# HGRN2 scores below level 16: elementwise products and whole-block matmuls, or 32 keys on each column tile against their own 32 queries

## Chip, core and metric

One core of a Trainium2 chip runs the whole program. The time is the device time of one execution in microseconds; the runs shown are three executions, and one more was taken with the hardware profiler.

## What is computed

One decoder layer for a prompt of 256 tokens with 16 meta tokens ahead of it, and for 8 sample tokens: a half-step SwiGLU, a mixer, a second half-step SwiGLU, all in fp32. The mixer projects x by `w_in` into ten parts and runs two recurrences side by side, retention (8 heads) and HGRN2 (16 heads of 128). The change is in HGRN2's scores inside a block:

```python
b = jnp.cumsum(logf.astype(jnp.float32), axis=2)
causal = jnp.tril(jnp.ones((C, C), dtype=bool))
diff = b[:, :, :, None, :] - b[:, :, None, :, :]
decay = jnp.exp(jnp.where(causal[None, None, :, :, None], diff, -jnp.inf)).astype(q.dtype)
A = jnp.einsum('bhid,bhjd,bhijd->bhij', q, k, decay)
o = jnp.einsum('bhij,bhjv->bhiv', A, v) + jnp.einsum('bhid,bhdv->bhiv', q * jnp.exp(b).astype(q.dtype), S)
```

The decay depends on the query i, the key j and the channel d, so A is no plain matrix product. `f` is the forget gate, `logf` its logarithm, `k` is 1 - f.

## The kernel before

All large products run as three matmuls of rounded halves (`dense`, L217: xh by whi, xl by whi, xh by wlo). Weights stream in units of eight 128x128 blocks: SyncE (SP) issues the load `raw` (L184, three buffers), ScalarE rounds it to `whi` (L187), VectorE subtracts for `wlo` (L188). TensorE's order is the order of the code; the other engines' order is set by a scheduler from priorities and readiness, and each engine then runs its list in order.

In the mixer, `project()` walks the columns of `w_in` in groups of two outputs: 16 steps of six matmuls each, four steps to a weight unit. After every step `pump` counts down the waiting threads and lets those go on whose count is over. There are eight rounds u; round u starts one `mix_hg(u)` (two HGRN2 heads) and one `mix_ret(u)` (a retention head), generators whose `yield n` means: go on after n steps of the projection. Small matmuls thus stand between dense ones at places that the yields fix. `calm` adds two steps to most waits in u=2 to 6 and in u=0.

`mix_hg` splits a block's scores into levels 1 to 64. At level s, a key in the even half of a pair of s-token pieces meets a query in the odd half; before each level, K and Q are scaled by products T of forget gates (T1 is f, T2s is the product of neighbours in Ts), so that a product of K and Q has the right decay. The scores are put together in `acch`, keys on partitions.

- Diagonal, levels 1 and 2: products of columns of Q and K made by VectorE (`pr0` to `pr2`, then `pr0`, `pr1`), each rounded into two halves (`prodsmh`, `prodvbh`, ScalarE and VectorE), and summed over the 128 channels by a matmul with ones (`sums`, L236). The sums come out the same on all partitions; the diagonal is cut out by a product with the identity (L789), level 1 by one and level 2 by two masked copies (L883, `copy_predicated`).
- Levels 4 and 8: 128 keys by 192 columns of `Qm`, an arrangement of Q's odd halves with three scalings (L801), four fp32 matmuls, then six masked copies (L805).
- Levels 16, 32 (L825) and 64 (L820): small matmuls on column tiles (`tile_position=(0, j)`), copied by ScalarE.

After that come K's transposes (L899), the samples' state update (smh, vbh, L905 and L906), the states, the samples' products `pq` (L932, column tiles too) and the outputs. In `mix_ret` the names used below are `pt` (transposes, L1006), `vbr` and `smr` (the samples' values, broadcast by a load in two halves, `spread(0)` and `spread(1)`, and the samples' states, L1037 and L1069; `vbr` has one buffer) and `pqr` (L1083), the products with `smr`.

Of the kernel before, what the change touches and what calls it, by code (L numbers as in the profile page):

```python
# [14 lines left out]
ALU = mybir.AluOpType  # L15
# [32 lines left out]
MASKS = {1: [0], 2: [1, MASKED], 4: [2], 8: [3, MASKED + 1]}  # L48
# [79 lines left out]
def trunk(ctx: ExitStack, tc: tile.TileContext, A, O):  # L128
# [417 lines left out]
    with tc.tile_pool(name="yp", bufs=1) as yp:  # L546
# [7 lines left out]
        with tc.tile_pool(name="mp", bufs=1) as mp:  # L554
# [178 lines left out]
            def mix_hg(u, f, k, q, v):  # L733
# [51 lines left out]
                yield 9  # L785
                pd = mx_bank("pd")
                sums(pd, hilo, slice(0, 2))
                for h in range(2):
                    nc.vector.tensor_tensor(  # L789
                        out=acc[:, 2 * P * h : 2 * P * (h + 1)].rearrange("p (b c) -> p b c", b=2),  # L790
                        in0=pd.rearrange("p (b c h) -> p h b c", b=2, h=2)[:, h],
                        in1=ident.unsqueeze(1).to_broadcast([P, 2, P]), op=ALU.mult)
                Tt = f
                for s in LEVELS:
                    if s == 4:


                        for h in range(2):
                            pl = mx_bank("pl")
                            for b in range(2):  # L800
                                nc.tensor.matmul(  # L801
                                    pl[:, 192 * b : 192 * b + 192], K[:, h, NMETA + b * P : NMETA + b * P + P],
                                    Qm.rearrange("p i (x c) -> p i x c", x=4)[:, :, 2 * h + b, :], start=True, stop=True)
                            for i, (sl, mi) in enumerate(((4, MASKS[4][0]), (8, MASKS[8][0]), (8, MASKS[8][1]))):
                                nc.vector.copy_predicated(  # L805
                                    acc[:, 2 * P * h : 2 * P * (h + 1)].rearrange("p (b n t s) -> p b n t s", b=2, t=2, s=sl)[:, :, :, 1, :],
                                    msk[:, mi, :P].rearrange("p (b n s) -> p b n s", b=2, s=sl),
                                    pl[:, :384].rearrange("p (b i n s) -> p b i n s", b=2, i=3, s=sl)[:, :, i])
# [19 lines left out]

                    if s == NMETA:
                        Tt = Tt[:, :, 1:]  # L830
                    k0 = 0 if s < NMETA else NMETA
                    n = LP - k0
                    nb = n // s
                    m = nb // 2
                    t2 = Tt[:, :, :nb].rearrange("p h (n t) -> p h n t", t=2)
                    kv = K[:, :, k0:].rearrange("p h (n t s) -> p h n t s", t=2, s=s)
                    qv = Q.rearrange("p h (n t s) -> p h n t s", t=2, s=s)
                    mq = SEQ // (2 * s)
                    mul(kv[:, :, :, 0, :], kv[:, :, :, 0, :], t2[:, :, :, 1].unsqueeze(3).to_broadcast([P, 2, m, s]))
                    if s != 4:  # L840
                        mul(qv[:, :, :, 1, :], qv[:, :, :, 1, :], t2[:, :, m - mq :, 0].unsqueeze(3).to_broadcast([P, 2, mq, s]))
                    Tn = tmp(f"T{2 * s}", (P, 2, m))
                    mul(Tn, t2[:, :, :, 0], t2[:, :, :, 1])
                    Tt = Tn
# [44 lines left out]
                    if s != 4:  # L889
                        yield W_LEVEL + 2 * (s <= 2 or u == 1) + calm  # L890
# [358 lines left out]
```

## Time and profile before

| what | us |
| --- | --- |
| runs (three): median, lowest, highest | 2610.65, 2608.11, 2611.9 |
| profiled execution | 2608.88 |
| its span in the trace | 2607.1 |
| TensorE busy in the span | 2586.9 |
| VectorE, ScalarE busy | 1723.9, 1385.2 |
| granted TensorE clock, mean | 0.999 |

The profiled execution is 1.8 us longer than its span, and 1.8 us shorter than the median of the runs. A row of a timeline gives the start, the duration (a matmul's end is modelled, so neighbours overlap), engine, line, operation and operands, then a count of the records in the row.

### The profile page before, as it was taken

What the parts mean: (1) busy time and instruction counts of PE and PEld (TensorE: products, weight loads), DVE (VectorE), ACT (ScalarE), POOL (GpSimd) and SP (SyncE); (2) the same over time, 40 slices, a digit from 0 to 9 for tenths busy, and PEclk for the clock granted to TensorE, in tenths of its full rate; (3) what the DMA queues carried; (4) which work ended last, traced back from release to release, by engine and by line L of the source; (5) the groups of instructions that cost most, each with busy time, mean ns of one, the idle gap of its engine ahead of it and who ended that gap; (6) DMA issues with size and microseconds to landing.
All of it is one profiled execution on the core that took longest, in us unless ns stands there. A gap on an engine that the chain in (4) does not pass through costs nothing.

```text
span 2607.1 us, 54875 instructions
## 1 busy us (share of the span) xinstructions
PE 2586.9 (99%) x22744; PEld 2554.0 (98%) x22744; DVE 1723.9 (66%) x2907; ACT 1385.2 (53%) x2184; POOL 12.9 (0%) x62
## 2 busy tenths in 40 slices
PE   9999999999999999999999999999999999999999
PEld 9999999999999889999999999999999999999998
DVE  6454444565579787777777777776995555556555
ACT  5444444444456666766666666675564444444444
POOL 0000000000000000000000000000000000000000
PEclk9999999999999999999999999999999999999999
DMA  7555555555556676767676767666556666666664
GB/s 244 183 185 186 186 183 184 185 185 184 183 198 222 219 260 205 262 202 260 206 260 201 262 202 259 207 228 194 193 188 200 195 195 196 196 196 193 199 196 147
DMA packets 154587, 536.17 MB, mean 206 GB/s; under 512 B 17696, under 2 KB 25696, under 8 KB 154336
## 3 DMA queue, kind: packets, MB, share of 16 engines
q1 hardware_dynamic: 154048, 532.37, 63.1%
q8 instruction: 178, 2.92, 0.5%
q14 instruction: 73, 0.60, 0.1%
q10 hardware_dynamic: 288, 0.29, 0.0%
HBM read 501.99 MB, written 30.61 MB: 204 GB/s over the span
## 4 chain that ended last, share of the span: by engine, by line
PE 92%; DVE 4%; DMA 2%; ACT 2%; issue 1%; SPq 0%; POOL 0%; DVEq 0%; POOLq 0%; ACTq 0%
PE up L217 36%; PE dn L217 18%; PE pj_q_r L217 3%; PE wo L217 3%; PE pj_v_r L217 3%; PE pj_i_h L217 3%; PE pj_f L217 3%; PE pj_k_r L217 3%; PE pj_g_r L217 3%; PE pj_q_h L217 3%; PE pj_a_r L217 3%; PE pj_g_h L217 3%; PE pj_a_h L217 3%; DVE wlo L188 1%; DMA out_srp<-sro 1%; PE pqr L1083 1%
## 5 line engine op out<-in xcount | busy, mean ns | idle before, releaser
L188 DVE TENSOR_TENSOR wlo<-raw,whi 128x1024 fp32r<-128x1024 f32 (+1 forms) x869 | 1061.6, 1222 | 735.1 <-ACT whi L187 732.8
L187 ACT CAST whi<-raw 128x1024 fp32r<-128x1024 f32 (+1 forms) x870 | 905.5, 1042 | 906.5 <-PE up L217 415.2
L217 PE MATMUL up<-xh,wlo 128*128 128x280 f32 (+1 forms) x2624 | 725.7, 280 | 0.3 <-DVE wlo L188 0.3
L217 PE MATMUL up<-xh,whi 128*128 128x280 f32 (+1 forms) x2624 | 726.0, 280 | 0.0
L217 PE MATMUL up<-xl,whi 128*128 128x280 f32 (+1 forms) x2624 | 725.4, 279 | 0.0
L217 PEld LDWEIGHTS up<-xh,wlo 128*128 128x128 f32 x2624 | 492.6, 189 | 0.7 <-DVE wlo L188 0.7
L217 PEld LDWEIGHTS up<-xh,whi 128*128 128x128 f32 x2624 | 493.1, 189 | 0.0
L217 PEld LDWEIGHTS up<-xl,whi 128*128 128x128 f32 x2624 | 492.7, 189 | 0.0
L217 PE MATMUL dn<-hh,whi 128*128 128x280 f32 (+1 forms) x1376 | 384.7, 280 | 0.0
L217 PE MATMUL dn<-hl,whi 128*128 128x280 f32 (+1 forms) x1376 | 384.3, 279 | 0.0
L217 PE MATMUL dn<-hh,wlo 128*128 128x280 f32 (+1 forms) x1376 | 384.3, 279 | 0.0
L217 PEld LDWEIGHTS dn<-hh,whi 128*128 128x128 f32 x1376 | 260.1, 189 | 0.1
L217 PEld LDWEIGHTS dn<-hl,whi 128*128 128x128 f32 x1376 | 260.1, 189 | 0.1
L217 PEld LDWEIGHTS dn<-hh,wlo 128*128 128x128 f32 x1376 | 260.1, 189 | 0.0
L217 PE MATMUL pj_g_r<-xh,whi 128*128 128x264 f32 x256 | 76.7, 299 | 0.0
L217 PE MATMUL pj_v_r<-xh,whi 128*128 128x280 f32 x256 | 74.2, 290 | 0.0
L217 PE MATMUL pj_g_h<-xh,whi 128*128 128x264 f32 x256 | 73.5, 287 | 0.0
L217 PE MATMUL pj_v_r<-xh,wlo 128*128 128x280 f32 x256 | 72.4, 283 | 0.3 <-DVE wlo L188 0.3
L217 PE MATMUL pj_k_r<-xh,whi 128*128 128x280 f32 x256 | 72.7, 284 | 0.0
L217 PE MATMUL pj_k_r<-xh,wlo 128*128 128x280 f32 x256 | 72.4, 283 | 0.0
L217 PE MATMUL pj_v_r<-xl,whi 128*128 128x280 f32 x256 | 72.3, 283 | 0.0
L217 PE MATMUL pj_k_r<-xl,whi 128*128 128x280 f32 x256 | 72.3, 283 | 0.0
(403 smaller groups left out, 5283.4 us busy)
## 6 DMA issues: line engine op xcount, KB each, us to landing
raw<-in_w_up SPq DMA_DIRECT2D x343, 512.0 KB, 4.2
raw<-in_w_in SPq DMA_DIRECT2D x320, 512.0 KB, 4.0
raw<-in_w_dn SPq DMA_DIRECT2D x172, 512.0 KB, 3.5
smr<-in_sr SPq DMA_DIRECT2D x32, 512.0 KB, 5.6
out_srs<-smr SPq DMA_DIRECT2D x32, 512.0 KB, 4.8
raw<-in_w_out SPq DMA_DIRECT2D x32, 512.0 KB, 3.6
smh<-in_sg SPq DMA_DIRECT2D x16, 512.0 KB, 4.4
vbr<-vrd SPq DMA_DIRECT2D x16, 512.0 KB, 4.4
```

The costliest lines, as they stand in the source:

```text
L187: nc.scalar.copy(hi[:, j:jn, :], raw[:, j:jn, :])
L188: nc.vector.tensor_tensor(out=lo[:, j0:j1, :], in0=raw[:, j0:j1, :], in1=hi[:, j0:j1, :].bitcast(F32), op=ALU.subtract)
L217: nc.tensor.matmul(o, w, t, start=start, stop=stop)
L1083: nc.tensor.matmul(pq[32 * j : 32 * j + 32, :256], qdr[:, c, 32 * b : 32 * b + 32], sms[2 * e + c][:, j, :], start=e + c == 0, stop=e + c ...
```

## The change

Levels 1 and 2 with the diagonal, and levels 4 and 8, are each one call of `blocks()`. It takes 32 keys on the column tile (0, j) and multiplies them with the three 16-column arrangements of their own 32 queries (L808, 48 moving columns); the first call also with the 32 queries as they are, for the diagonal (L810, 32 columns). Each head's results lie in one bank and are taken by a product with the identity for the diagonal (L815, first call alone) and three masked copies of 128 elements a partition (L821). `side_by_side` (two ScalarE copies and two VectorE scalings) makes the arrangement for each call. K is scaled by f and T2 only after the first call, by T4 and T8 after the second. The products `pr`, their halves and `sums` over them are gone, and so is the extra wait of two steps after levels 1 and 2: the calls stand 14 and 27 steps after the start of the thread where `calm` is 2, level 16 at 39 as before. The two masks of level 2 change places in the table.

```diff
-MASKS = {1: [0], 2: [1, MASKED], 4: [2], 8: [3, MASKED + 1]}
+MASKS = {1: [0], 2: [MASKED, 1], 4: [2], 8: [3, MASKED + 1]}
...
-                hilo = [tmp("prod" + t, (P, 3, SEQ), dt=F32R, tag=t, bufs=2) for t in ("smh", "vbh")]
-                for i in range(3):
-                    pr = tmp(f"pr{i}", (P, SEQ))
-                    if i < 2:
-                        mul(pr, q[:, i, :SEQ], k[:, i, NMETA:LP])
-                    else:
-                        mul(pr.rearrange("p (h c) -> p h c", h=2), Q[:, :, 1::2], K[:, :, NMETA::2])
-                    split(hilo[0][:, i], hilo[1][:, i], pr)
+                Ts = {1: f}
+                def sides(s):
+                    k0 = 0 if s < NMETA else NMETA
+                    m = (LP - k0) // (2 * s)
+                    Tt = Ts[s] if k0 == 0 or s > NMETA else Ts[s][:, :, 1:]
+                    return k0, m, Tt[:, :, : 2 * m].rearrange("p h (n t) -> p h n t", t=2)
+                def scale_k(s):
+                    k0, m, t2 = sides(s)
+                    x = K[:, :, k0:].rearrange("p h (n t s) -> p h n t s", t=2, s=s)[:, :, :, 0, :]
+                    mul(x, x, t2[:, :, :, 1].unsqueeze(3).to_broadcast([P, 2, m, s]))
+                def odd(s):
+                    return Q.rearrange("p h (n t s) -> p h n t s", t=2, s=s)[:, :, :, 1, :]
+                def scale_q(s):
+                    _, m, t2 = sides(s)
+                    n = SEQ // (2 * s)
+                    mul(odd(s), odd(s), t2[:, :, m - n :, 0].unsqueeze(3).to_broadcast([P, 2, n, s]))
+                def join(s):
+                    _, m, t2 = sides(s)
+                    Ts[2 * s] = tmp(f"T{2 * s}", (P, 2, m))
+                    mul(Ts[2 * s], t2[:, :, :, 0], t2[:, :, :, 1])
+                def side_by_side(s):
+                    x = tmp("Qm", (P, 3, 2 * P), tag="smh", bufs=2)
+                    part = lambda i, s: x[:, i, :].rearrange("p (h n s) -> p h n s", h=2, s=s)
+                    nc.scalar.copy(part(0, s), odd(s))
+                    scale_q(s)
+                    nc.scalar.copy(part(1, 2 * s), odd(2 * s))
+                    k0 = NMETA // s
+                    t4 = Ts[s][:, :, k0 : k0 + SEQ // s].rearrange("p h (n t) -> p h n t", t=4)[:, :, :, 1]
+                    mul(part(2, 2 * s), odd(2 * s), t4.unsqueeze(3).to_broadcast([P, 2, SEQ // (4 * s), 2 * s]))
+                    return x
+                def blocks(x, s, own=None):
+                    x = x.rearrange("p i (x j c) -> p i x j c", x=4, j=4)
+                    for h in range(2):
+                        pl = mx_bank("pl")
+                        half = pl[:, : 2 * 80].rearrange("p (b c) -> p b c", b=2)
+                        for b in range(2):
+                            for j in range(0, P, 32):
+                                kk = K[:, h, NMETA + b * P + j : NMETA + b * P + j + 32]
+                                o = half[j : j + 32, b, :48].rearrange("p (i c) -> p i c", i=3)
+                                nc.tensor.matmul(o, kk, x[:, :, 2 * h + b, j // 32, :], start=True, stop=True, tile_position=(0, j))
+                                if own is not None:
+                                    nc.tensor.matmul(
+                                        half[j : j + 32, b, 48:], kk, own[:, h, b * P + j : b * P + j + 32],
+                                        start=True, stop=True, tile_position=(0, j))
+                        a = acc[:, 2 * P * h : 2 * P * (h + 1)]
+                        if own is not None:
+                            nc.vector.tensor_tensor(
+                                out=a.rearrange("p (b j c) -> p b j c", b=2, j=4),
+                                in0=half[:, :, 48:].unsqueeze(2).to_broadcast([P, 2, 4, 32]),
+                                in1=ident.rearrange("p (j c) -> p j c", j=4).unsqueeze(1).to_broadcast([P, 2, 4, 32]), op=ALU.mult)
+                        for i, (sl, mi) in enumerate(((s, MASKS[s][0]), (2 * s, MASKS[2 * s][0]), (2 * s, MASKS[2 * s][1]))):
+                            n = 16 // sl
+                            nc.vector.copy_predicated(
+                                a.rearrange("p (b j n t s) -> p b j n t s", b=2, j=4, t=2, s=sl)[:, :, :, :, 1, :],
+                                msk[:, mi, :P].rearrange("p (b j n s) -> p b j n s", b=2, j=4, s=sl),
+                                half[:, :, 16 * i : 16 * i + 16].rearrange("p b (n s) -> p b n s", s=sl).unsqueeze(2).to_broadcast([P, 2, 4, n, sl]))
+                join(1)
+                Q1 = side_by_side(1)
...
-                yield 9
-                pd = mx_bank("pd")
-                sums(pd, hilo, slice(0, 2))
-                for h in range(2):
-                    nc.vector.tensor_tensor(
-                        out=acc[:, 2 * P * h : 2 * P * (h + 1)].rearrange("p (b c) -> p b c", b=2),
-                        in0=pd.rearrange("p (b c h) -> p h b c", b=2, h=2)[:, h],
-                        in1=ident.unsqueeze(1).to_broadcast([P, 2, P]), op=ALU.mult)
-                Tt = f
-                for s in LEVELS:
-                    if s == 4:
-                        for h in range(2):
-                            pl = mx_bank("pl")
-                            for b in range(2):
-                                nc.tensor.matmul(
-                                    pl[:, 192 * b : 192 * b + 192], K[:, h, NMETA + b * P : NMETA + b * P + P],
-                                    Qm.rearrange("p i (x c) -> p i x c", x=4)[:, :, 2 * h + b, :], start=True, stop=True)
-                            for i, (sl, mi) in enumerate(((4, MASKS[4][0]), (8, MASKS[8][0]), (8, MASKS[8][1]))):
-                                nc.vector.copy_predicated(
-                                    acc[:, 2 * P * h : 2 * P * (h + 1)].rearrange("p (b n t s) -> p b n t s", b=2, t=2, s=sl)[:, :, :, 1, :],
-                                    msk[:, mi, :P].rearrange("p (b n s) -> p b n s", b=2, s=sl),
-                                    pl[:, :384].rearrange("p (b i n s) -> p b i n s", b=2, i=3, s=sl)[:, :, i])
-                    elif s != 8:
-                        pl = mx_bank("pl")
-                    if s == 1:
-                        sums(pl[:, :SEQ], hilo, 2)
-                    elif s == 2:
-                        sums(pl, hilo)
-                    for h in range(2 if s > 8 else 0):
+                yield 10 + calm
+                blocks(Q1, 1, q)
+                scale_q(2)
+                join(2)
+                Q4 = side_by_side(4)
+                scale_k(1)
+                scale_k(2)
+                yield 2 * W_LEVEL - 1 + calm
+                blocks(Q4, 4)
+                join(4)
+                for s in (4, 8):
+                    scale_k(s)
+                scale_q(8)
+                join(8)
+                yield W_LEVEL + 4 + 2 * (u == 1) + calm
+                for s in LEVELS[MASKED:]:
+                    pl = mx_bank("pl")
+                    for h in range(2):
                         for b in range(2):
                             k0, q0, o = NMETA + b * P, b * P, (2 * h + b) * s
                             if s == 64:
...
-                    if s == 1:
-                        q4 = Q.rearrange("p h (n t i) -> p h n t i", t=2, i=2)[:, :, :, 1, :]
-                        hilo = [tmp("prod" + t, (P, 2, SEQ), dt=F32R, tag=t, bufs=2) for t in ("smh", "vbh")]
-                        for j in range(2):
-                            pr = tmp(f"pr{j}", (P, SEQ))
-                            mul(pr.rearrange("p (h n i) -> p h n i", h=2, i=2), q4,
-                                K[:, :, NMETA + j :: 4].unsqueeze(3).to_broadcast([P, 2, SEQ // 4, 2]))
-                            split(hilo[0][:, j], hilo[1][:, j], pr)
-                    if s == 2:
-                        Qm = tmp("Qm", (P, 3, 2 * P), tag="smh", bufs=2)
...
-                    else:
-                        x = pl.rearrange("p (c j) -> p j c", j=2) if s == 2 else pl.rearrange("p (j c) -> p j c", j=2)
-                        for j, mi in enumerate(MASKS[s]):
-                            nc.vector.copy_predicated(
-                                acc.rearrange("p (n t s) -> p n t s", t=2, s=s)[:, :, 1, :],
-                                msk[:, mi, :].rearrange("p (n s) -> p n s", s=s),
-                                x[:, j].rearrange("p (n s) -> p n s", s=s))
                     if s in (16, 32):
                         load(s // 32)
-                    if s != 4:
-                        yield W_LEVEL + 2 * (s <= 2 or u == 1) + calm
+                    yield W_LEVEL + 2 * (u == 1) + calm
+                Tt = Ts[2 * LEVELS[-1]]
```

TensorE, round u=2, the sums of the diagonal and level 1 before (`pd` and `pl` are PSUM banks, `prodsmh` and `prodvbh` the halves):

```order
L217 MATMUL pj_q_r5_12263<-xl1_13_9281,whi79_12403 128x264
L217 MATMUL pj_q_r5_12263<-xh1_13_9280,wlo79_12404 128x264
L236 MATMUL pd_12420<-prodsmh_12301,ones_r_79 128x512
L236 MATMUL pd_12420<-prodvbh_12302,ones_r_79 128x512
L236 MATMUL pl_12425<-prodsmh_12301,ones_r_79 128x256
L236 MATMUL pl_12425<-prodvbh_12302,ones_r_79 128x256
L217 MATMUL pj_q_r4_12262<-xh1_14_9284,whi79_12403 128x264
L217 MATMUL pj_q_r4_12262<-xl1_14_9285,whi79_12403 128x264
```

and the start of the first `blocks` call after:

```order
L217 MATMUL pj_k_r5_12475<-xl1_0_9229,whi80_12477 128x280
L217 MATMUL pj_k_r5_12475<-xh1_0_9228,wlo80_12478 128x280
L808 MATMUL pl_12488<-Qm_12343,K_12332 32x48
L810 MATMUL pl_12488<-q_12160,K_12332 32x32
L808 MATMUL pl_12488<-Qm_12343,K_12332 32x48
L810 MATMUL pl_12488<-q_12160,K_12332 32x32
L808 MATMUL pl_12488<-Qm_12343,K_12332 32x48
L810 MATMUL pl_12488<-q_12160,K_12332 32x32
```

Four sums of 512 and 256 columns give way to 32 matmuls of 48 and 32 columns in turn, two on a tile and then two on the next; they stand three steps later.

Levels 4 and 8 in round u=2, before and after:

```order
L217 MATMUL pj_v_r5_12610<-xl1_1_9233,whi84_12612 128x280
L217 MATMUL pj_v_r5_12610<-xh1_1_9232,wlo84_12613 128x280
L801 MATMUL pl_12629<-Qm_12533,K_12292 128x192 x2
L801 MATMUL pl_12635<-Qm_12533,K_12292 128x192 x2
L217 MATMUL pj_v_r4_12609<-xh1_2_9236,whi84_12612 128x280
L217 MATMUL pj_v_r4_12609<-xl1_2_9237,whi84_12612 128x280
```

```order
L217 MATMUL pj_k_r5_12475<-xl1_13_9281,whi83_12619 128x280
L217 MATMUL pj_k_r5_12475<-xh1_13_9280,wlo83_12620 128x280
L808 MATMUL pl_12636<-Qm_12533,K_12332 32x48 x8
L808 MATMUL pl_12648<-Qm_12533,K_12332 32x48 x8
L217 MATMUL pj_k_r4_12474<-xh1_14_9284,whi83_12619 128x280
L217 MATMUL pj_k_r4_12474<-xl1_14_9285,whi83_12619 128x280
```

Four matmuls of 192 columns by 128 keys become 16 of 48 columns by 32 keys, with no second product between them.

VectorE, round u=0, around the scaling of K by T8 that level 16 needs (`wlo30` to `wlo32` are low halves of weight units, `smr` the retention samples' states), before:

```order
L239 TENSOR_TENSOR K_9490<-K_9490,T4_9782 128x68x4
L188 TENSOR_TENSOR wlo31_10065<-raw31_10063,whi31_10064 128x8x128
L239 TENSOR_TENSOR K_9490<-K_9490,T8_9950 128x34x8
L239 TENSOR_TENSOR T4_11071<-T2_10982 128x136
L239 TENSOR_TENSOR T8_11173<-T4_11071 128x68
L1069 SCALAR_TENSOR_TENSOR smr_9679<-vbr_9801,k_r_9445,smr_9679 128x256 x3
L188 TENSOR_TENSOR wlo32_10102<-raw32_10100,whi32_10101 128x8x128
L1069 SCALAR_TENSOR_TENSOR smr_9679<-vbr_9801,k_r_9445,smr_9679 128x256
L1069 SCALAR_TENSOR_TENSOR smr_9681<-vbr_9801,k_r_9445,smr_9681 128x256 x4
```

and after:

```order
L821 COPY_PREDICATED acch_9498<-msk_88,pl_9864 128x16x8
L821 COPY_PREDICATED acch_9498<-msk_88,pl_9876 128x16x8
L239 TENSOR_TENSOR K_9490<-K_9490,T4_9683 128x68x4
L254 TENSOR_TENSOR vs2_8641<-vt2_8636,vs2_8641 24x256
L239 TENSOR_TENSOR K_9490<-K_9490,T8_9888 128x34x8
L188 TENSOR_TENSOR wlo30_10026<-raw30_10024,whi30_10025 128x8x128
```

The scaling by T8 stood behind the low half of unit 31 and now stands behind that of unit 29.

VectorE, round u=1, where the retention samples' states `smr` are updated with the second half of `vbr`; before:

```order
L188 TENSOR_TENSOR wlo64_11757<-raw64_11755,whi64_11756 128x8x128
L254 TENSOR_TENSOR km_8638<-ptk_11614,km_8638 16x128
L1069 SCALAR_TENSOR_TENSOR smr_11384<-vbr_11413,k_r_10677,smr_11384 128x256 x4
L1069 SCALAR_TENSOR_TENSOR smr_11386<-vbr_11413,k_r_10677,smr_11386 128x256
L188 TENSOR_TENSOR wlo65_11787<-raw65_11785,whi65_11786 128x8x128
L1069 SCALAR_TENSOR_TENSOR smr_11386<-vbr_11413,k_r_10677,smr_11386 128x256 x3
L254 TENSOR_TENSOR km_8638<-ptk_11652,km_8638 16x128
L239 TENSOR_TENSOR gt_11743<-gs_11742,pj_g_h1_11527 128x264
L188 TENSOR_TENSOR wlo66_11832<-raw66_11830,whi66_11831 128x8x128
```

and after:

```order
L188 TENSOR_TENSOR wlo64_11797<-raw64_11795,whi64_11796 128x8x128
L254 TENSOR_TENSOR km_8638<-ptk_11654,km_8638 16x128
L254 TENSOR_TENSOR km_8638<-ptk_11692,km_8638 16x128
L188 TENSOR_TENSOR wlo65_11827<-raw65_11825,whi65_11826 128x8x128
L239 TENSOR_TENSOR gt_11783<-gs_11782,pj_g_h1_11567 128x264
L1070 SCALAR_TENSOR_TENSOR smr_11424<-vbr_11453,k_r_10697,smr_11424 128x256
L188 TENSOR_TENSOR wlo66_11872<-raw66_11870,whi66_11871 128x8x128
L1070 SCALAR_TENSOR_TENSOR smr_11424<-vbr_11453,k_r_10697,smr_11424 128x256 x3
L1070 SCALAR_TENSOR_TENSOR smr_11426<-vbr_11453,k_r_10697,smr_11426 128x256 x4
L239 TENSOR_TENSOR gt_11783<-gt_11783,gs_11786 128x264
```

Of the four updates of each state, five in all stood ahead of the low half of unit 65 and three behind it; now one stands ahead of that of unit 66 and seven behind it.

SP, the same place: the load of the second half of `vbr` before and after.

```order
L184 DMA raw65_11785<-in_w_in 128x1024
L1072 DMA out_srs<-smr_11133 128x1024
L1037 DMA vbr_11413<-vrd_11250 128x1024
L184 DMA raw66_11830<-in_w_in 128x1024
L184 DMA raw67_11887<-in_w_in 128x1024
L1072 DMA out_srs<-smr_11384 128x1024
```

```order
L184 DMA raw65_11825<-in_w_in 128x1024
L1073 DMA out_srs<-smr_11192 128x1024
L184 DMA raw66_11870<-in_w_in 128x1024
L184 DMA raw67_11927<-in_w_in 128x1024
L1038 DMA vbr_11453<-vrd_11290 128x1024
```

It moved from ahead of the load of unit 66 to behind that of unit 67.

More of the change, by code (lines that the diff above doesn't have):

```diff
@@ L827, in mix_hg @@
                                         Q[:, h, q0 + j + s : q0 + j + 2 * s], start=True, stop=True, tile_position=(0, j))
[L829 to L836, printed above, removed]
@@ L837, in mix_hg @@
-                    qv = Q.rearrange("p h (n t s) -> p h n t s", t=2, s=s)
-                    mq = SEQ // (2 * s)
-                    mul(kv[:, :, :, 0, :], kv[:, :, :, 0, :], t2[:, :, :, 1].unsqueeze(3).to_broadcast([P, 2, m, s]))
-                    if s != 4:
-                        mul(qv[:, :, :, 1, :], qv[:, :, :, 1, :], t2[:, :, m - mq :, 0].unsqueeze(3).to_broadcast([P, 2, mq, s]))
-                    Tn = tmp(f"T{2 * s}", (P, 2, m))
-                    mul(Tn, t2[:, :, :, 0], t2[:, :, :, 1])
@@ L854, in mix_hg @@
-                    if s == 2:
-                        Qm = tmp("Qm", (P, 3, 2 * P), tag="smh", bufs=2)
-                        qf = Q.rearrange("p h c -> p (h c)")
-                        odd = [qf.rearrange("p (n t s) -> p n t s", t=2, s=sl)[:, :, 1, :] for sl in (4, 8)]
-                        nc.scalar.copy(Qm[:, 0, :].rearrange("p (n s) -> p n s", s=4), odd[0])
-                        t4 = Tt[:, :, NMETA // 4 :].rearrange("p h (n t) -> p h n t", t=2)[:, :, :, 0]
-                        q4 = Q.rearrange("p h (n t s) -> p h n t s", t=2, s=4)[:, :, :, 1, :]
-                        mul(q4, q4, t4.unsqueeze(3).to_broadcast([P, 2, 32, 4]))
-                        nc.scalar.copy(Qm[:, 1, :].rearrange("p (n s) -> p n s", s=8), odd[1])
-                        t4 = Tt[:, :, NMETA // 4 :].rearrange("p h (n t) -> p h n t", t=4)[:, :, :, 1]
-                        mul(Qm[:, 2, :].rearrange("p (h n s) -> p h n s", h=2, s=8),
-                            Q.rearrange("p h (n t s) -> p h n t s", t=2, s=8)[:, :, :, 1, :],
-                            t4.unsqueeze(3).to_broadcast([P, 2, 16, 8]))
@@ L868, in mix_hg @@
-                    if s in (4, 8):
-                        pass
-                    elif s == 64:
+                    scale_k(s)
+                    scale_q(s)
+                    join(s)
+                    if s == 64:
                         for b in range(2):
@@ L874, in mix_hg @@
                                 pl[b * s : (b + 1) * s, : 2 * s].rearrange("p (h s) -> p h s", h=2))
-                    elif s >= 16:
+                    else:
                         for j in range(0, 128 // s, 2):
```

2 lines of the change are left out of this document (removed), and 2 rows, old and new, of the table rows.

## The prediction

> **What bounds the kernel now.** I read the page first, its busy shares and its chain of waits.
>
> ```profile
> span 2607.1 us, 54875 instructions
> PE 2586.9 (99%) x22744; PEld 2554.0 (98%) x22744; DVE 1723.9 (66%) x2907; ACT 1385.2 (53%) x2184; POOL 12.9 (0%) x62
> PE 92%; DVE 4%; DMA 2%; ACT 2%; issue 1%; SPq 0%; POOL 0%; DVEq 0%; POOLq 0%; ACTq 0%
> ```
>
> TensorE is busy for 99% of the span and is 92% of the chain. The mixer is where the change lies, so the same question goes to it: the windows view over one of its eight rounds, then over the 40 us of that round in which the low levels are done.
>
> ```profile
> 1142.50:1272.50 130.00, 130.00 (x1187) 126.53 (x1186) 101.11 (x204) 83.13 (x158) 1.21 (x3) 1.00 0.72 232
> 1145.00:1185.00 40.00, 40.00 (x378) 39.51 (x376) 32.08 (x66) 23.88 (x52) 0.00 (x0) 1.00 0.75 249
> ```
>
> The columns after the stretch are its length, then PE, PEld, DVE, ACT and POOL, then clock, DMA share and GB/s. TensorE has no gap, VectorE a fifth of the time free, ScalarE over a third, the clock is full. So in this stage **only what TensorE executes, and what it waits for, is paid**. A group of small matmuls costs what it pushes the next dense matmul back.
>
> **What TensorE does at the changed places.** The timeline of TensorE in round u=2, around each of the old groups:
>
> ```profile
> 1151.70 0.28 PE L217 MATMUL pj_q_r<-xh,wlo 128*128 128x264 f32 x1
> 1151.81 0.38 PE L236 MATMUL pd<-prodsmh,ones_r 128*128 128x512 f32 x1
> ...
> 1152.48 0.28 PE L217 MATMUL pj_q_r<-xh,whi 128*128 128x264 f32 x1
> 1152.59 0.28 PE L217 MATMUL pj_q_r<-xl,whi 128*128 128x264 f32 x1
> ...
> 1159.43 0.28 PE L217 MATMUL pj_k_r<-xh,wlo 128*128 128x280 f32 x1
> ...
> 1160.10 0.28 PE L217 MATMUL pj_k_r<-xl,whi 128*128 128x280 f32 x1
> ...
> 1167.01 0.28 PE L217 MATMUL pj_v_r<-xh,wlo 128*128 128x280 f32 x1
> 1167.13 1.46 PE L801 MATMUL pl<-Qm,K 128*128 128x192 f32 x8
> 1168.30 0.42 PE L217 MATMUL pj_v_r<-xh,whi 128*128 128x280 f32 x1
> 1168.55 0.28 PE L217 MATMUL pj_v_r<-xl,whi 128*128 128x280 f32 x1
> ```
>
> Dense matmuls start 0.11 us apart (1152.48 to 1152.59). I measure a group from the start of the last dense one ahead of it to the start of the second one behind it, less two such steps (0.22). The sums of the diagonal and level 1 push by 0.89 - 0.22 = **0.67 us**, those of level 2 (between 1159.43 and 1160.10) by 0.67 - 0.22 = **0.45**, the eight records of levels 4 and 8 by 1.54 - 0.22 = **1.32**. Together 2.44 us in a round, all of it removed.
>
> What comes has no row of its own: keys of 32 columns, four column tiles, 48 or 32 moving columns. Its nearest rows are the groups that use column tiles already.
>
> ```profile
> 1180.19 0.28 PE L217 MATMUL pj_a_r<-xh,wlo 128*128 128x264 f32 x1
> 1180.40 0.45 PE L825 MATMUL pl<-Q,K 128*32 128x32 f32 x16
> ...
> 1180.99 0.28 PE L217 MATMUL pj_g_r<-xl,whi 128*128 128x264 f32 x1
> ...
> 1220.78 0.28 PE L217 MATMUL pj_a_r<-xh,wlo 128*128 128x264 f32 x1
> 1220.98 1.08 PE L932 MATMUL pq<-smh,qdh 128*32 128x128 f32 x32
> ...
> 1222.21 0.28 PE L217 MATMUL pj_g_r<-xl,whi 128*128 128x264 f32 x1
> ```
>
> Level 32 (two tiles, 16 records) pushes by 0.80 - 0.22 = 0.58 us; the samples' products (four tiles, 32 records of 128 columns) by 1.43 - 0.22 = 1.21. A moving column's price comes from L801: 1.32 us by 8 records of 192 columns is 0.86 ns a column and record (an fp32 matmul is two records). One after another, 32 records of 128 columns would be 32 x 0.110 = 3.5 us; they took 1.21. Eight sets of four at once are 8 x 0.110 = 0.88, and 0.33 is left: what it costs to go from whole-array matmuls to column tiles and back. Level 32 agrees: 8 sets of two x 0.0275 = 0.22, 0.36 left. So **four column tiles do run at once, for about 0.34 us a group**. The same group cut after its first tenth of a microsecond shows it directly:
>
> ```profile
> L932 PEld LDWEIGHTS pq<-smh,qdh x8: 106/108/109, 1221.0 to 1221.0; 128*32 128x32 f32 x8
> L932 PE MATMUL pq<-smh,qdh x4: 297/297/297, 1221.0 to 1221.0; 128*32 128x128 f32 x4
> ```
>
> Four matmuls have started and eight sets of weights were fetched: each tile has its second record's weights behind the first.
>
> **The sum on TensorE.** *Stage 2* (levels 4 and 8): 32 records of 48 columns, 8 sets of four, the two records of one matmul in a row on a tile as in L932: 8 x 0.041 + 0.34 = **0.67 us**. *Stage 1*: 32 records of 48 and 32 of 32 columns; wholly at once 8 x 0.041 + 8 x 0.0275 + 0.34 = 0.89. But here four records in a row fall on one tile (48, 48, 32, 32), and no row shows whether the instructions for the next tile get past the third and fourth. If the third waits until the second has started, each of the 16 bursts holds the queue for one record: 16 x 0.041 + 0.34 = **1.00**; if the fourth waits for the third's start as well, 16 x 0.082 + 0.34 = 1.65; strictly one after another, 32 x 0.041 + 32 x 0.0275 + 0.34 = 2.53, and stage 2 then 32 x 0.041 + 0.34 = 1.65. I take 1.00, nearest to the fetch-ahead that L932 shows. The sum is 1.67 instead of 2.44, **-0.77 us a round, -6.2 us for eight**; the ends are 1.56 (-7.0 us) and 4.18 (+13.9 us).
>
> The page "TensorE: Matmul & The Clock Gate" of the Trainium skill, Part 3, The mechanism, speaks against this change: it has matmuls starting and ending strictly in program order, so that a tile's second record would hold up the next tile's first. By it the sum would be that of rival E below; four starts inside a tenth of a microsecond in L932, whose tiles' second records stand between them in the program, do not look like it.
>
> **VectorE and ScalarE** lose work. Rows of the groups by line, over all rounds:
>
> ```profile
> L883 DVE COPY_PREDICATED acch<-msk,pl 128x256 f32<-128x256 uint8 x24 | 17.6, 733 | 3.6 <-PE pl L236 3.5
> L225 DVE TENSOR_TENSOR prodvbh<-pr,prodsmh 128x256 fp32r<-128x256 f32 x40 | 15.7, 417 | 0.0
> L805 DVE COPY_PREDICATED acch<-msk,pl 128x128 f32<-128x128 uint8 x48 | 11.3, 290 | 0.0
> L239 DVE TENSOR_TENSOR pr<-Q,K 128x256 f32<-128x256 f32 x24 | 9.6, 421 | 0.2
> ```
>
> A round drops five products (0.42), five lower halves (0.42) and three masked copies (0.73), 6.4 us, and gains six masked copies (0.29) and one scaling (0.42), 2.2: -4.2 us of VectorE, hidden by TensorE's 130 us, so worth nothing directly. ScalarE drops five casts and gains two copies, hidden too. The swapped masks of level 2 cost nothing: same two copies. The new chain (blocks 1, eight evictions, two key scalings, blocks 4) has 13 dense steps of six matmuls between its stages, 13 x 6 x 0.112 = 8.7 us, for 2 x 0.42 + 6 x 0.29 + 2 x 0.42 = 3.4 us of VectorE and one or two weight halves of 1.14 us (the chain below) among them; it fits, so I book no wait for u of 2 and up.
>
> **Waits.** The waits view of TensorE has few, all in the first two rounds but for a part of the first line:
>
> ```profile
> PE pqr L1083 <- DVE smr L1069: 3.0, 3, 1.9
> PE pl L825 <- DVE Q L239: 1.6, 1, 1.6
> PE pt L1006 <- DVE acch L805: 1.5, 1, 1.5
> PE pl L825 <- DVE K L239: 0.7, 1, 0.7
> ```
>
> The two of L825 (levels 32 and 16 in u=0) come from scalings that stand behind a weight half of the unit after the one TensorE is in; in the new order they stand one and two halves earlier. The wait of 1.5 is for a PSUM bank that the levels 4 and 8 evictions release; stage 2 now runs three steps ahead of that transpose. Together 3.8 us; I book -3.5.
>
> Against it stands pqr in u=1. VectorE's waits for the load in question, the page's row of its issues (size, and median us to landing), then the chain and SP's timeline there:
>
> ```profile
> DVE smr L1069 <- DMA vbr<-vrd: 16.1, 8, 2.6
> ...
> vbr<-vrd SPq DMA_DIRECT2D x16, 512.0 KB, 4.4
> ...
> 960.61 6.28 DMA vbr<-vrd
> 966.92 0.50 DVE smr L1069
> ...
> 968.98 1.14 DVE wlo L188
> 970.12 0.40 DVE smr L1069
> ...
> 970.57 1.41 PE pqr L1083 x6
> ...
> 962.45 2.28 SPq L184 DMA_DIRECT2D raw<-in_w_in  x2
> ```
>
> The second vbr load is issued at 960.61, ahead of raw66; in the new order it stands behind raw67, whose issue ends 962.45 + 2.28 = 964.7. VectorE's products wait for it, with the weight halves queued behind them, and TensorE at pqr waits for the products. After the landing came 2.06 + 1.14 + 1.26 us and pqr's last part; now one product, the half wlo66 and seven products, 0.2 us more. Issued between 962.8 and 964.7, landing in 4.4 (the page's median) to 6.3 us, it ends 0.3 to 4.1 us later, 0.5 to 4.3 with the longer tail: I take **+2.5**. Waits net: -1.0 us.
>
> **Forecast.** The profiled execution ran 2608.9 us (span 2607.1 and 1.8 around it): 2608.9 - 6.2 - 1.0 = 2601.7. The median of the runs shown, 2610.65, lies 1.8 above that execution, so the new median should be 2610.65 - 7.2 = **2603.4 us**. About 0.2% (5.2 us) is what a measurement of this kernel can tell from no change.
>
> **Rivals.** (A) *A tile's burst holds the queue* for two records: stage 1 is 1.65, the sum 2.32, so -1.0 us for the eight rounds and -1.0 for waits: 2608.7. For it: two sets of weights a tile is all that L932 shows. Against it: nothing but the choice of depth. (B) *The vbr load decides*: TensorE gains its 6.2, pqr in u=1 grows by 4.3 and of the early waits only half goes (-1.9): 2610.65 - 3.8 = 2606.9. For it: all eight rounds of the page's groups have VectorE waiting for this load. (C) *Slower: nothing runs at once.* In bursts of four on one tile the records run one after another, stage 1 costs 2.53 and stage 2 1.65: 2610.65 + 13.9 - 1.0 = 2623.6. It is slower than before from the point where the two stages cost over 2.44 + 6.2 / 8 = 3.2 us. Against it: L932, whose bursts of two overlap. (D) *The change does less than it says*: each set is limited by its weight fetches and not by the moving columns. Level 32's 0.58 us for 16 records bounds this at 0.015 us a record beyond the 0.34; 96 records give 96 x 0.015 + 0.68 = 2.12, so -2.6 and -1.0: 2607.1. (E) *Starts in program order*: only a burst's last record runs beside the next tile's first; stage 1 is 16 x (0.041 + 0.041 + 0.0275) + 0.34 = 2.09, stage 2 16 x 0.041 + 0.34 = 1.00, together 3.09, +5.2 and -1.0: 2614.9. Against it: L932 by it would push 16 x 0.110 + 0.34 = 2.1 us, and it pushes 1.21.
>
> **Chances.** Forecast 0.56; A 0.16; B 0.09; C 0.05; D 0.10; E 0.04. A, B, D and half of E lie within 0.2%, and of the forecast's own width (2600 to 2607, the ends of stage 1 and of the waits) some 0.04 does too: faster 0.52, same 0.41, slower 0.07. The range for 8 in 10 goes from 2599 (sum 1.56, all early waits gone, pqr not later) to 2610 (A, with pqr at its upper end).
>
> **What would show it.** Right: L808 and L810 groups whose records start in sets of four, pushing by about 1.0 and 0.67 us; TensorE's waits on L825 and on the bank gone; pqr in u=1 ending 2 to 3 us later after its scores; VectorE some 34 us less busy. Wrong: a stage 1 over 1.6 us (A), a longer stage 2 too (C or D), a new TensorE wait on K in u of 2 and up (the 13 steps too short), or pqr waits that move in the other rounds.

## The result and the profile after

The changed kernel takes 2605.53 us (median of 22 runs) against 2609.80 of the kernel before (22 runs): ratio 0.9985, 95% interval 0.9978 to 0.9992, so 4.3 us faster. 2603.4 was forecast, 7.2 us less than the median of the three runs shown; the sign and the range held, and the gain is inside the 0.2% that I had called hard to tell from nothing.

The page of the changed kernel, busy times and chain, then its TensorE waits (line waited at, releaser, us in all, times, longest):

```profile
span 2606.2 us, 56106 instructions
PE 2580.9 (99%) x23400; PEld 2546.5 (98%) x23400; DVE 1703.7 (65%) x2859; ACT 1375.4 (53%) x2160; POOL 13.7 (1%) x62
PE 92%; DVE 4%; DMA 2%; ACT 1%; issue 1%; SPq 0%; POOL 0%; ACTq 0%; POOLq 0%; DVEq 0%
```

```profile
PE pqr L1084 <- DVE smr L1070: 9.9, 3, 5.2
PE up L217 <- DVE wlo L188: 1.3, 4, 0.6
...
PE up L217 <- ACT whi L187: 1.0, 1, 1.0
```

Nothing has taken TensorE's place as the bound. The waits of levels 16 and 32 and for the bank are gone; that at pqr rose from 3.0 to 9.9 us. Of the 2.3 us on `up`, 1.9 lie in the first 40 us, ahead of every changed instruction, and put the mixer's projection 1.9 us later than in the execution of the kernel before; the rest was there before. This execution ran 2608.29 us, 2.8 above the median, so stretches of the two traces are compared from the projection on.

The new groups on TensorE in one of the rounds, each between its dense neighbours:

```profile
1288.32 0.28 PE L217 MATMUL pj_k_r<-xh,wlo 128*128 128x280 f32 x1
1288.54 0.31 PE L808 MATMUL pl<-Qm,K 128*32 128x48 f32 x8
1288.64 0.25 PE L810 MATMUL pl<-q,K 128*32 128x32 f32 x7
1288.70 0.21 PE L808 MATMUL pl<-Qm,K 128*32 128x48 f32 x1
1288.71 0.20 PE L810 MATMUL pl<-q,K 128*32 128x32 f32 x1
1288.72 0.28 PE L808 MATMUL pl<-Qm,K 128*32 128x48 f32 x6
...
1289.38 0.39 PE L217 MATMUL pj_k_r<-xh,whi 128*128 128x280 f32 x1
...
1298.66 0.28 PE L217 MATMUL pj_k_r<-xh,wlo 128*128 128x280 f32 x1
1298.87 0.55 PE L808 MATMUL pl<-Qm,K 128*32 128x48 f32 x32
1299.35 0.39 PE L217 MATMUL pj_k_r<-xh,whi 128*128 128x280 f32 x1
1299.57 0.28 PE L217 MATMUL pj_k_r<-xl,whi 128*128 128x280 f32 x1
```

Measured as in the prediction, with 0.24 for two dense steps (these of 280 columns start 0.12 us apart), stage 2 pushes by 1299.57 - 1298.66 - 0.24 = 0.67 us. Behind stage 1 the second dense matmul starts at 1289.60, so it pushes by 1289.60 - 1288.32 - 0.24 = 1.04 us; over all rounds the mean is the same. In the program two L808 records and two L810 records alternate tile by tile; in the trace eight L808, two for each of the four tiles, have started before the first L810. So a tile's third record waits and the other tiles' first ones go past it.

Where the time went, by stretches of each kernel's one trace (all by the starts of TensorE's records): up to the first matmul of the projection; from there to the last record of pqr in u=1; to the first matmul of w_out (rounds u=2 to 7); and pqr itself, first to last record, whose least is 1.56. The rows below the first two are the experiments of the next section.

| kernel | median us | to projection | to end of pqr u=1 | u=2 to 7 | pqr u=0, u=1 | pqr u=2 to 7, sum |
| --- | --- | --- | --- | --- | --- | --- |
| before | 2609.8 | 744.7 | 226.9 | 832.2 | 6.0, 5.4 | 15.4 |
| changed | 2605.5 | 746.6 | 229.9 | 826.4 | 8.5, 10.7 | 13.0 |
| vbh_before | 2608.8 | 744.8 | 234.3 | 825.5 | 1.6, 1.6 | 9.3 |
| vbh_after | 2600.3 | 744.9 | 227.7 | 822.8 | 1.6, 1.6 | 9.3 |
| prio_before | 2602.4 | 744.7 | 222.0 | 828.8 | 1.6, 4.5 | 10.4 |
| prio | 2594.6 | 744.9 | 220.1 | 826.0 | 3.0, 3.4 | 11.4 |
| prio_u1 | 2597.1 | 746.1 | 221.8 | 823.8 | 9.1, 3.2 | 11.1 |
| own_last | 2605.2 | 745.2 | 227.9 | 827.0 | 8.6, 9.5 | 14.0 |
| stage1_only | 2615.7 | 744.8 | 225.1 | 842.6 | 5.7, 8.7 | 21.7 |
| stage2_only | 2612.0 | 744.8 | 228.3 | 835.5 | 4.8, 9.7 | 19.0 |
| gam_before | 2618.2 | 745.6 | 222.0 | 843.8 | 2.9, 4.2 | 15.8 |
| gam_after | 2615.0 | 745.4 | 218.4 | 842.1 | 1.6, 3.2 | 15.0 |
| gam_stage1 | 2627.0 | 744.7 | 220.5 | 856.6 | 1.6, 3.5 | 14.3 |
| gam_prio_own_last | 2616.2 | 744.9 | 218.4 | 844.6 | 1.6, 1.6 | 9.4 |

The rest, from w_out to TensorE's last start, is 796.8 to 796.9 us in all of them. The changed kernel gained 5.8 us in u=2 to 7 and lost 2.9 in u=0 and 1. That is 2.9 us for these two executions, where the medians differ by 4.3; the changed kernel's own runs lie between 2602.8 and 2609.7.

### The profile page after: what moved, and what is told of

The parts are those of the page before. It is cut to its first block, busy times and chain, and to the rows that moved or that the text cites. A ratio compares the mean times of both kernels' runs of the same rounds, so it can differ in the third digit from the quotient of the medians.

```text
span 2606.2 us, 56106 instructions
## 1 busy us (share of the span) xinstructions
PE 2580.9 (99%) x23400; PEld 2546.5 (98%) x23400; DVE 1703.7 (65%) x2859; ACT 1375.4 (53%) x2160; POOL 13.7 (1%) x62
## 4 chain that ended last, share of the span: by engine, by line
PE 92%; DVE 4%; DMA 2%; ACT 1%; issue 1%; SPq 0%; POOL 0%; ACTq 0%; POOLq 0%; DVEq 0%
PE up L217 35%; PE dn L217 18%; PE pj_f L217 4%; PE pj_q_h L217 3%; PE wo L217 3%; PE pj_k_r L217 3%; PE pj_v_r L217 3%; PE pj_g_r L217 3%; PE pj_i_h L217 3%; PE pj_q_r L217 3%; PE pj_a_r L217 3%; PE pj_g_h L217 3%; PE pj_a_h L217 3%; DVE wlo L188 2%; DMA vbr<-vrd 1%; PE pqr L1084 1%
## 5 line engine op out<-in xcount | busy, mean ns | idle before, releaser
L188 DVE TENSOR_TENSOR wlo<-raw,whi 128x1024 fp32r<-128x1024 f32 (+1 forms) x869 | 1062.4, 1223 | 748.6 <-ACT whi L187 745.4
```

Of the source, the lines that this page charges most:

```text
L188: nc.vector.tensor_tensor(out=lo[:, j0:j1, :], in0=raw[:, j0:j1, :], in1=hi[:, j0:j1, :].bitcast(F32), op=ALU.subtract)
```

## The experiments

Theory P: the two stages save TensorE some 5.5 us, and what u=0 and 1 lose is the second vbr load, on which pqr waits. Rival Q: the stages save little; the gain is VectorE's relief.

**A second buffer for vbr, in both kernels.**

```diff
-                    vbs.append(tmp("vbr", (P, 4, 256)))
+                    vbs.append(tmp("vbr", (P, 4, 256), tag="vbh" if e else None, bufs=2 if e else 1))
```

> The kernel before, with the second half of vbr in a buffer of its own (one of the two that vbh uses), so that its load no longer waits for the updates with the first half. Theory P (the waits at pqr are the vbr load's): the load is issued some four weight units earlier, pqr takes 1.6 to 2 us in each round instead of 2.0 to 6.0, and the time falls by 8 to 14 us against the kernel before. Rival Q (pqr waits for VectorE's own backlog, or for the states' load): pqr stays within 1 us of what it was, the time within 3 us.

> The same edit on the changed kernel. Theory P: with the load out of the way nothing gives back what the stages and the early waits of u=0 and u=1 save, so it lies 7 to 10 us below the same edit on the kernel before (5.5 from the two stages, 2 to 4 from waits), and 13 to 20 us below the changed kernel. Rival Q (the stages save little, the gain is VectorE's relief): it lies 4 us or less below the other one.

vbh_before took 2608.79 us (ratio to before 0.9996, 0.9988 to 1.0005), vbh_after 2600.33 (0.9963, 0.9950 to 0.9975). The pair differs by 8.5 us, as P expected and more than Q allowed. But the edit by itself gained nothing, where I expected 8 to 14, and 5.2 us on the changed kernel, where I expected 13 to 20: pqr went to its least in every round, and u=0 and 1 lost much of it again. TensorE's waits in vbh_before:

```profile
PE pl L825 <- DVE Q L239: 6.0, 1, 6.0
PE ptk L899 <- DVE K L239: 5.5, 1, 5.5
```

The updates with vbr had moved ahead of scalings of Q and K in VectorE's list, and level 32's scores in u=0 and K's transposes in u=1 waited in pqr's place. vbh_after has the same two waits, 5.3 and 5.9 us. In u=2 to 7 the pair differs by less than 3 us, where the two stages push by 4.1 us less in six rounds: new waits at other places took a part back, of `pt` for POOL (0.5 us) and of `pl` for a scaling of Q (0.3) among them.

**Priority for the vbr loads: all of them (in both kernels), and one alone.** The second form has the priority only where u == 1 and e == 1.

```diff
-                    nc.sync.dma_start(vbs[e], vrow[4 * e : 4 * e + 4, :].partition_broadcast(P))
+                    with tc.high_priority():
+                        nc.sync.dma_start(vbs[e], vrow[4 * e : 4 * e + 4, :].partition_broadcast(P))
```

> The changed kernel with the issue of the vbr loads at high priority: in SP's list the second load of u=1 moves from behind raw67 to ahead of raw65, that of u=0 two units up, the others one place at most. Theory P: pqr in u=1 falls from 10.7 us to 4 to 7, in u=0 from 8.5 to 6 to 8, the time by 4 to 7 us against the changed kernel. Rival Q: no change beyond 2 us.

> The changed kernel with high priority for one load alone, the second half of vbr in u=1: it goes from behind raw67 to ahead of raw65, all else in SP's list as in the changed kernel. Theory P (u=1's place of this load is what the changed kernel pays): pqr in u=1 falls from 10.7 us to about 3.4, as where all vbr loads had priority, pqr in u=0 stays near 8.5; the time falls by 6 to 8 us against the changed kernel, to about 2598. Rival Q (the gain of all priorities came from u=0 and the later rounds): at most 3 us.

> The kernel before with all vbr issues at high priority: in SP's list the second load goes two units up in u=0, from behind out_srs and raw65 to ahead of raw65's store in u=1, one place in the others. Theory P: pqr shrinks in u=0 and in the later rounds, less in u=1, and what the change is worth beside the same edit is its stages and early waits, 7 to 11 us: 2594.6 + 9 = about 2603. Rival Q (the stages save little): within 4 us of the changed kernel with the same edit, 2599 or less.

prio took 2594.59 us (0.9945, 0.9933 to 0.9957), prio_u1 2597.14 (0.9950, 0.9936 to 0.9963), prio_before 2602.44 (0.9971, 0.9959 to 0.9982). prio gained 10.9 us on the changed kernel, more than the 4 to 7 I expected: pqr in u=0 and u=1 fell to 3.0 and 3.4 us. One load's place in u=1 is worth about 8 us: with it alone pqr there fell from 10.7 to 3.2 us, with u=0 left at 9.1. Here are both, the chain of waits of the changed kernel first, of prio second:

```profile
963.89 7.71 DMA vbr<-vrd
...
972.02 1.22 DVE wlo L188
973.24 0.41 DVE smr L1070
...
973.69 3.35 PE pqr L1084 x14
```

```profile
954.27 6.10 DMA vbr<-vrd
...
961.98 1.22 DVE wlo L188
963.20 0.41 DVE smr L1071
...
963.65 1.81 PE pqr L1085 x8
```

The load is issued 9.6 us earlier, and pqr's last stretch starts 10 us earlier, of which 1.7 us lie ahead of the projection. The pair prio_before and prio differs by 7.9 us, again P's and not Q's size; their two profiled executions differ by 4.1 only, so the traces do not show where the rest lies. prio is the fastest version here, 0.55% below the kernel before and 0.4% below the changed one.

**The order within stage 1.** All four tiles' 48-column matmuls, then the four of 32 columns:

```diff
-                            for j in range(0, P, 32):
+                            for mine in (False,) if own is None else (False, True):
+                                for j in range(0, P, 32):
```

> The changed kernel with the order of stage 1 changed alone: the four tiles' 48-column matmuls first, then the four tiles' 32-column ones, so that two records in a row fall on a tile and not four. Theory P (a tile's third record holds the queue until its second has started): stage 1 pushes by 0.85 to 0.92 us instead of 1.04, 1 to 1.5 us off the time. Rival R (the sets are limited by fetches or by the switch): stage 1 stays at 1.04, the time the same.

2605.24 us (0.9985, 0.9976 to 0.9994); the time shows no difference from the changed kernel, where I expected 1 to 1.5 us, TensorE's rows do:

```profile
1285.43 0.28 PE L217 MATMUL pj_k_r<-xh,wlo 128*128 128x280 f32 x1
1285.64 0.29 PE L814 MATMUL pl<-Qm,K 128*32 128x48 f32 x8
1285.75 0.24 PE L810 MATMUL pl<-q,K 128*32 128x32 f32 x8
...
1286.61 0.28 PE L217 MATMUL pj_k_r<-xl,whi 128*128 128x280 f32 x1
```

Sets of eight now follow each other in order at first, and the group pushes by 1286.61 - 1285.43 - 0.24 = 0.94 us. Four records in a row on a tile cost 0.1 us a round: P is right in kind, R (1.04) falls, though 0.94 stays above the 0.85 to 0.92 expected. Eight rounds of it are 0.8 us, too little for the time to show.

**Each stage alone.** stage2_only keeps products and sums and puts the 32-key matmuls in L801's place; stage1_only keeps L801's matmuls with the new stage 1, and here is its edit of the changed kernel:

```diff
-                blocks(Q4, 4)
+                for h in range(2):
+                    pl = mx_bank("pl")
+                    for b in range(2):
+                        nc.tensor.matmul(
+                            pl[:, 192 * b : 192 * b + 192], K[:, h, NMETA + b * P : NMETA + b * P + P],
+                            Q4.rearrange("p i (x c) -> p i x c", x=4)[:, :, 2 * h + b, :], start=True, stop=True)
...
```

> Levels 1 and 2 and the diagonal by the new stage, levels 4 and 8 by 128 keys and 192 columns as before. By the trace of the changed kernel the new stage pushes by 1.04 us against 0.67 + 0.43: 0.5 us less in eight rounds. In SP's list u=1's vbr load stands one unit further up than in the changed kernel, with five updates ahead of wlo66. Theory P: the rounds u=2 to 7 take as long as before within 1.5 us, and the time lies between 2606 and 2612. Rival Q (VectorE's relief is the gain; it is all in this part): 2604 to 2606, as the changed kernel.

> Levels 4 and 8 by the new stage, the rest as before (products and sums for the diagonal and levels 1 and 2). Its 0.67 us against 1.30 is 5.0 us less in eight rounds. u=1's vbr load and the updates stand as in the changed kernel, behind raw67 and around wlo66. Theory P: u=2 to 7 are 3 to 5 us shorter than before, pqr in u=1 takes 8 to 11 us, and the time lies at 2605 to 2610. Rival Q: as the kernel before, 2609 to 2612, with rounds u=2 to 7 unchanged.

Both halves are slower than before, the second barely: stage1_only 2615.66 us (1.0030, 1.0018 to 1.0042), stage2_only 2612.00 (1.0011, 1.0002 to 1.0020). P's times missed in both, and stage2_only's is that of Q, though not for Q's reason, since the rounds did change: both expectations on u=2 to 7 missed, with 10.4 and 3.4 us more than before. The groups themselves cost what they cost in the whole change (1.04 us; 0.67 us); pqr grew by 6.3 and 3.6 us over the six rounds, though the vbr load and the updates stand at the same places in SP's and VectorE's lists as before. In stage1_only ScalarE's waits for the samples' states show more:

```profile
ACT smh L916 <- DMA smh<-in_sg: 44.5, 15, 6.3
```

These waits are 28.0 us in the changed kernel and 17.2 in the one before. In ScalarE's list one scaling of the second head's state stands ahead of a weight cast there, and behind it in the changed kernel. That this makes the weights late is argued from list and waits, not tried alone. It can't be the cause in stage2_only, where these waits are 17.5 us; what made its pqr longer stays open.

**The start of the chain to pqr.** The chain of the changed kernel in u=1 has, ahead of the updates, a store and the write of gam, which lies in the buffer of sro:

```profile
946.35 6.12 DMA out_srp<-sro
952.67 0.11 POOL sro L1062
952.80 1.16 ACT smr L1067
```

Theory S: this store starts the chain, in the halves too. gam got a tile of its own, in four kernels.

```diff
-                gam = tmp("sro", (P, 1))
+                gam = tmp("gam", (P, 1))
```

> The kernel before, with the scalar gam in a tile of its own and no longer in the buffer of sro. Theory S (the chain to pqr starts when the store out_srp has landed, since gam is written into its buffer; then come ScalarE's scaling, the updates, the second vbr load, the updates): the scalings start 0.5 to 1.3 us earlier in u=2 to 7 and 3 to 4 us earlier in u=0 and 1, pqr takes under 2.2 us in u=2 to 7, the time falls by 6 to 12 us, to 2598 to 2604. Rival V (the vbr load's own place alone): pqr in u=2 to 7 as before (15.4 us in all), the time within 4 us.

> The same edit on the changed kernel; u=1's vbr load and updates then stand in the same places as in gam_before. Theory P (with equal order at pqr the change is worth its stages and early waits): 5 to 9 us below gam_before, with the stages 5.5 us of it. Rival Q: within 3 us of it.

> The same edit on the kernel that has the new stage 1 alone. Theory S: the 6 us that this half lost against before, at pqr in u=2 to 7 (21.7 against 15.4 us), go, since the store that came later no longer starts the chain; the time lies within 3 us of gam_before, 0.5 us of stages and up to 2 us of early waits in its favour. Rival V or another cause: it stays 4 us or more above gam_before.

> The changed kernel with all three: gam in its own tile, vbr loads at high priority, the 32-column matmuls of stage 1 behind the four of 48 columns. Theory S and P: pqr at its floor of 1.6 us in u=2 to 7, 4 us less than with priority alone, and 0.75 us less in stage 1, so 2589 to 2593. Against that stands that with the load this early the updates went ahead of level 32's scalings in u=0 and 1 where vbr had a second buffer, and cost 5 us each there: 2594 to 2600 if they do so here.

All four came out slower than the kernel before: gam_before 2618.17 us (1.0028, 1.0018 to 1.0039), gam_after 2614.98 (1.0020, 1.0011 to 1.0029), gam_stage1 2626.96 (1.0069, 1.0055 to 1.0082) and gam_prio_own_last 2616.24 (1.0026, 1.0016 to 1.0035). I had expected 2598 to 2604 for the first and 2589 to 2600 for the last. S falls as to u=2 to 7: the updates of the first half came some 7 us earlier (in u=3, 20.8 us ahead of pqr for 13.1), and pqr stayed at 15.8 us, since the load behind them in SP's list keeps its place. In u=0 and 1 it did help (2.9 and 4.2 instead of 6.0 and 5.4). What it broke lies behind ScalarE. Its rows in gam_before, u=3:

```profile
1220.97 0.38 ACT L936 COPY osh<-pq 128x256 f32<-128x256 f32 x1
1226.60 1.15 ACT L1066 ACTIVATE smr<-smr,gam 128x1024 f32<-128x1024 f32 x1 [5.25 <-issue]
1227.65 0.37 ACT L680 ACTIVATE gs<-pj_g_r 128x264 f32<-128x264 f32 x1
1227.92 1.03 ACT L187 CAST whi<-raw 128x1024 fp32r<-128x1024 f32 x1
```

Free of sro, the scaling stands earlier in ScalarE's list. It waits 5.25 us, by its place for its state, whose load was issued at 1219.83 and had landed at 1226.53, and a weight cast stands behind it. TensorE's dense matmuls then wait for weights, first view. In gam_prio_own_last it waits more for a copy that ScalarE makes of the samples' products, second view:

```profile
PE pj_g_h L217 <- DVE wlo L188: 4.9, 8, 0.8
```

```profile
PE po L729 <- ACT osh L939: 10.1, 5, 3.1
```

The pair gam_before and gam_after differs by 3.2 us, less than P's 5 to 9 and just over Q's 3. In u=2 to 7 it differs by 1.7 us: the wait for ScalarE's copy is 3.1 us in gam_after and 1.6 in gam_before, which covers a part of the stages' 4.1. gam_stage1 lies 8.8 us above gam_before, so the half's loss was not the store's doing; its cause stays open.

## Why the prediction was right, and where it missed

- **TensorE's stages.** Predicted 1.00 and 0.67, measured 1.04 and 0.67; before, 1.10 and 1.30 as a mean of the rounds (1.12 and 1.32 in the prediction, which took 0.22 for two steps of 280 columns too). That is 0.68 us a round, 5.5 for eight (4.1 in u=2 to 7), against 6.2 forecast. Four tiles at once, with 0.34 us for going to column tiles and back, give stage 2 to the hundredth. A, C and E fall by the trace, since stage 1 of 1.65, 2.53 or 2.09 was not seen, and D since the two stages are 1.71 and not 2.12. The way to the 1.00 was wrong, though, and its number lucky. If each burst held the queue for one record, the eighth L808 would start 4 x 0.041 = 0.16 us after the first, behind the first L810; but eight started within 0.10 us (1288.54 to 1288.64), ahead of any L810. Of the 0.15 us above 0.89, the sum for all at once, own_last's order saves 0.1; how the rest comes about stays open. In the pairs vbh and prio the change is worth 8.5 and 7.9 us, about the sum of this and the early waits; that it is made of them is argued, since u=2 to 7 of those traces show less than 3 us each and not 4.1.
- **VectorE and ScalarE.** Busy 20.2 and 9.8 us less; I had booked 34 for VectorE. Products and halves took 32.0 us off (15.7, 9.6 and 6.7 in the rows), but the masked copies only 1.1 (17.6 and 11.3 before, 27.8 in the row below): all twelve of a round take 383 ns now, where I had booked 290. The identity's product and the new scaling added 4.4. The 8.5 us that are left are small growth of many rows and time that two rows share, which the page's total counts once. All of it hidden, as forecast.

```profile
L821 DVE COPY_PREDICATED acch<-msk,pl 128x128 f32<-128x128 uint8 x96 | 27.8, 383 | 0.1
```

- **The early waits** went, all of them, but -3.5 us was wrong as a gain. Counted from the projection's first matmul, TensorE reached pqr in u=0 4.0 us sooner (at 859.3 before and 857.2 now in the traces), but the second vbr load landed only 1.8 us sooner, and pqr took 8.5 us for 6.0. So 2.5 of the 4.0 us were given back there. I had named the load as what is late next in u=1 alone; pqr waits that move in the other rounds were the prediction's own sign of being wrong, and they came. VectorE's products behind that load, before and now:

```profile
861.73 3.26 DVE L1069 SCALAR_TENSOR_TENSOR smr<-vbr,k_r,smr 128x256 f32<-128x256 f32 x8 [1.38 <-DMA vbr<-vrd]
```

```profile
861.88 3.25 DVE L1070 SCALAR_TENSOR_TENSOR smr<-vbr,k_r,smr 128x256 f32<-128x256 f32 x8 [2.97 <-DMA vbr<-vrd]
```

- **pqr in u=1**, +2.5 (0.5 to 4.3): it grew by 5.2 us (10.65 for 5.41). The place in SP's list was right and prio_u1 shows that it is the cause; the size failed, since the load took 7.71 us, beyond the 4.4 to 6.3 I had taken as ends. Why it took so long is not shown; in prio it took 6.10. This step and that of u=0 cost the forecast about as much, 2.7 and 2.5 us.
- **Rival B** is nearest to what happened: 2606.9 was its time, 3.8 us less than before for the 4.3 measured. Its condition, a load that decides while the stages gain nearly in full, is what the runs showed. I gave it 0.09 because I counted the load's place in one round and not that u=0 stands on it too.
- **u=2 to 7** gained 5.8 us: 4.1 from the stages and 2.4 at pqr, which I had not booked, with 0.7 lost at other places, 0.5 of it in a new wait of `pt` for POOL. The 2.4 us were luck: they made up for about half of the 5.2 us by which the two steps above missed, and in the halves pqr went the other way, by 3.6 and 6.3 us.

## What to carry to other kernels

Where one engine is the bound and another queue feeds a later wait of it, a microsecond saved ahead of that wait can be given back there, as 2.5 of 4.0 us were in u=0; look in the chain for the next transfer whose landing moves less than what you save, and fix its place in the queue with the change. Judge such a change with that wait shortened in both kernels too: 4.3 us became 8.5 and 7.9 in two such pairs, though only 3.2 in the third, where the edit made new waits. And a wait that looks idle may hold an instruction back from a place in an in-order queue where it blocks others: taking it out cost 8 to 11 us here in three of the four kernels that it was tried in, counted from the kernel that each was made from. The fourth, which has prio's and own_last's edits as well, lies 21.6 us above prio.

## What the runs showed of the hardware

Matmuls on different column tiles do not start in program order here: in stage 1 eight L808 records started (1288.54) ahead of the first L810 (1288.64), which stands third in the program, and own_last's other order pushes by 0.94 us instead of 1.04. The Trainium skill, page "TensorE: Matmul & The Clock Gate", Part 3, The mechanism, has starts strictly in order; this trace does not agree with it across column tiles.
